# Where the second pass's features are transposed: score and value banks of PSUM in place of the products' ring, and a lead-in of six weave steps

## The chip, the core and the metric

The kernel runs on one core of one Trainium2 chip. The metric is the device time of one execution in microseconds; a measurement is the median of several executions. TensorE (PE in the profile) does the matrix products and the transposes, VectorE (DVE) and ScalarE (ACT) the elementwise work, GpSimd (POOL) a few subtractions, and the SP queue issues most of the transfers.

## What is computed

One layer of a hybrid step: attention and a matrix-memory scan side by side, one output projection, then a feed-forward network. There are 9 blocks of 128 tokens, one of context and eight latent ones, with a width of 1024. The parts that matter here are the last two of the layer:

```python
x = x + g1 * mix                          # mix: output projection of attention and scan
h2 = rmsnorm(x, norm2_w) * (1 + sc2) + sh2
x = x + g2 * swiglu(h2, w_gu, w_down)     # (silu(h2 @ w_g) * (h2 @ w_u)) @ w_down
```

## The kernel before

**Two passes of the feed-forward network.** The 9 blocks make 3 chunks of 3 blocks: `cur`, `nxt` and `far`. The feed-forward network of `cur` runs first, group by group of hidden columns: `gate_up` (24 products of 384 columns for each of two accumulators, lines 1473 to 1475 in `products`) and `down` (lines 1215 to 1217 in `three_blocks`). The chunks `nxt` and `far` follow together in a second pass, `pair6`, which forms a product of 2x2 blocks with seven block products in place of eight. It reads its right-hand operands, seven of them as pairs of fp16 parts, from the tile `Bt`.

**The features.** `Bt` is filled by `features6`, once for each of the six blocks of `nxt` and `far`. For each half of a block's 1024 columns it scales 512 columns on ACT into a buffer `t2` (line 1554), transposes them on PE in four pieces into a bank of PSUM (line 124, through the helper `transpose`), and copies the bank out with scale and shift into `F`: one quarter on ACT (line 1562), three on DVE (line 1564). Then ACT casts and DVE subtracts to make the two parts (lines 1569 and 145); a block of `far` also forms four sums T1 to T4 with its partner of `nxt` (lines 1578 to 1585).

**What runs beside it.** While groups of `cur` (from the fourth on) occupy PE, the generator `weave` takes side steps in proportion: first nothing for some steps, then the three blocks of `nxt`, then `attn_out` for `far` (its loads of spilled attention outputs into `t2` at line 1416, casts at 1418, products `out` at lines 1251 to 1255 and gated sums at 1204 and 1205, then row statistics at 1436 and the inverse root at 135 to 141), then the three blocks of `far`. The last heads of the attention for `far` (scores at line 1129, value products at 1153 and 1154) are still running as the first features come up. The program order made so is then moved by a scheduler, in which a `hot(n)` block goes ahead of other work by n.

**Banks.** PSUM has eight banks here: three for the attention's scores (`psum["S"]`, one tile of three banks), one for its value products (`psum["po"]`), and four that every other product takes in turn through `bank()`: gate-up, down, output projection, and the features' transposes.

**Buffers.** `t2` is a ring of three buffers of 2 KB a partition. The features' scaled halves, the gated sums, the loads at line 1416 and the scratch output of the weights' absolute sums (`jk`, line 178 in `load_piece`) share it. `F` and `T` lie in memory that the attention has used, so no `F` can be written before the attention's last output is through.

Of the kernel before, what the change touches and what calls it, by code (L numbers as in the profile page):

```python
# [8 lines left out]
F32 = mybir.dt.float32  # L9
# [10 lines left out]
P = 128  # L20
# [16 lines left out]
GROUPS = [(0, 4), (4, 4), (8, 4), (12, 5), (17, 5)]  # L37
# [5 lines left out]
NG = 3  # L43
# [6 lines left out]
def hybrid_step(ctx: ExitStack, tc: tile.TileContext, I: dict, O: dict):  # L50
# [8 lines left out]
    def hot(n):  # L59
        return tc.high_priority(n)  # L60

    def nm(s):
        uid[0] += 1
        return f"{s}_{uid[0]}"

    def weave(main, side, n_main, n_side):

        due = 0.0
        for units in main:
            due += n_side / n_main * (units or 1)  # L70
            while due >= 1.0:
                next(side, None)
                due -= 1.0

    def emit(gen):
        for _ in gen:
            pass

    def chain(*gens):
        for g in gens:  # L80
            for v in g:
                yield v
# [22 lines left out]
    psum = {"mm": es_b.enter_context(tc.tile_pool(name="pB", bufs=4, space=PSUM, reuse_waits="tile"))}  # L105
# [3 lines left out]
    def bank():  # L109
        turn_of[0] += 1  # L110
        at = psum["mm"] if "mm1" not in psum or turn_of[0] % 4 else psum["mm1"]
        return at.tile([P, 512], F32, name=nm("mm"), tag="mm")
# [10 lines left out]
    def transpose(out, in_, n=P):  # L123
        nc.tensor.transpose(out, in_, ident[:n, :n])
# [19 lines left out]
    def sub(out, full, hi, eng):  # L144
        (dve if eng == "dve" else pool).tensor_tensor(out=out, in0=full, in1=hi, op=ALU.subtract)  # L145
# [194 lines left out]
    ps = bank()  # L340
# [3 lines left out]
    ps = bank()  # L344
# [853 lines left out]
    def t2():  # L1198
        return ft.tile([P, 512], F32, name=nm("t2"), tag="t2", bufs=nt2[0])
# [206 lines left out]
    def attn_out(a, oT, row, home, spilled=None):  # L1406

        gs = row_pair(row)
        x1, parts = a["x1"], []
        for i in range(CB):  # L1410
            th, tl = home(i)
            parts.append((th, tl))
            o = oT[i]
            if spilled:
                o = t2().rearrange("p (k x) -> p k x", k=4)
                dma(o, spilled[i].rearrange("p (k x) -> p k x", k=4))
            with hot(500):
                nc.scalar.copy(th, o)
                sub(tl, o, th.bitcast(F32), "dve")
        for n in range(2):  # L1420
            with nullcontext() if spilled else tc.issue_after(loaded["turned"]):
                ws = out_pieces(0, n)
            for i, (th, tl) in enumerate(parts):
                ps = out_block([ws], 0, th, tl)
                with hot(200):
                    add_gated(x1[i], ps, gs[n], n)
                yield
        with hot(200):
            a["rs"] = stats(x1)
        yield  # L1430
# [46 lines left out]
    def gate_up(a, f0, nf):  # L1477
        th, tl = a["h2"]
        acts = a["act"] = []
        for f in range(f0, f0 + nf):  # L1480
            if True:
                pg, pu = bank(), bank()
                for off, ps in ((0, pg), (D_FF, pu)):
                    src = w_gu[f + (NF if off else 0)].rearrange("p (k n) -> p k n", k=KD)
                    wh, wl = load_piece([(full_view, src)], (KD, P), tally=2 * f + (off > 0))
                    products(ps[:, 0:CT], wh, wl, th, tl)
                    yield 6
                parts = [(slice(0, CT), pg[:, 0:CT], pu[:, 0:CT])]
            tn = fp.tile([P, CT], F32, name=nm("tn"), tag="tn", bufs=2)
            for cs, g, u in parts:  # L1490
                act(tn[:, cs], g, AF.Tanh, scale=0.5)
                dve.scalar_tensor_tensor(out=tn[:, cs], in0=tn[:, cs], scalar=1.0, in1=u, op0=ALU.add, op1=ALU.mult)  # L1492
                dve.tensor_tensor(out=tn[:, cs], in0=tn[:, cs], in1=g, op=ALU.mult)
            hl = hlp.tile([P, 2, CT], F32R, name=nm("hl"), tag="hl", bufs=5)
            ah, al = hl[:, 0], hl[:, 1]
            nc.scalar.copy(ah, tn)  # L1496
            sub(al, tn, ah.bitcast(F32), "pool")
            acts.append((ah, al))

    def down(c, a, f0, nf, n):  # L1500
        g = gate_bc(1, c, n)
        acts = a["act"]
        pieces = []
        for j in range(0, nf, 2):
            m = min(2, nf - j)
            rows = w_down[(f0 + j) * P : (f0 + j + m) * P, n * 512 : (n + 1) * 512].rearrange("(a p) n -> p a n", p=P)
            pieces.append(load_piece([(full_view, rows)], (m, 512)))
        yield from three_blocks(
            lambda k, i: (acts[k][0][:, i * P : (i + 1) * P], acts[k][1][:, i * P : (i + 1) * P]),
            pieces, nf, lambda i, ps: add_gated(a["x1"][i], ps, g(c * CB + i), n))  # L1510
# [35 lines left out]
    def features6(a, c, i, Bt, firsts):  # L1546

        x1, r = a["x1"][i], a["rs"][i]
        at = slice(i * P, (i + 1) * P)
        F = a4p.tile([P, KD, P], F32, name=nm("F"), tag="A4", bufs=7)  # L1550
        for half in range(2):
            with hot(600):
                y = t2()
                act(y, x1[:, half * 512 : (half + 1) * 512], AF.Copy, scale=r)
                ps = bank()
                for j in range(4):
                    transpose(ps[:, j * P : (j + 1) * P], y[:, j * P : (j + 1) * P])
                for j in range(4):
                    k = half * 4 + j
                    s, t = mods6[:, k, 0:1], mods6[:, k, 1:2]  # L1560
                    if j == 0:
                        act(F[:, k], ps[:, j * P : (j + 1) * P], AF.Identity, scale=s, bias=t)
                    else:
                        dve.tensor_scalar(out=F[:, k], in0=ps[:, j * P : (j + 1) * P], scalar1=s, scalar2=t, op0=ALU.mult, op1=ALU.add)
            yield
        for half, b in ((0, B11), (1, B21)) if c == 1 else ((1, B22),):
            v = F[:, half * 4 : half * 4 + 4]
            with hot(600):
                nc.scalar.copy(Bt[:, b, 0, :, at], v)
                sub(Bt[:, b, 1, :, at], v, Bt[:, b, 0, :, at], "dve")  # L1570
            yield
        if c == 1:
            firsts.append(F)
            return
        first = firsts.pop(0)
        T = sp.tile([P, 4, 4, P], F32, name=nm("T"), tag="S", bufs=1)
        with hot(600):
            dve.tensor_tensor(out=T[:, T1], in0=first[:, 0:4], in1=F[:, 0:4], op=ALU.subtract)
            dve.tensor_tensor(out=T[:, T2], in0=F[:, 4:8], in1=T[:, T1], op=ALU.add)
            dve.tensor_tensor(out=T[:, T3], in0=F[:, 0:4], in1=F[:, 4:8], op=ALU.subtract)  # L1580
            dve.tensor_tensor(out=T[:, T4], in0=first[:, 4:8], in1=T[:, T2], op=ALU.subtract)
        yield
        for j in (0, 2):
            with hot(600):
                nc.scalar.copy(Bt[:, j : j + 2, 0, :, at], T[:, j : j + 2])
                sub(Bt[:, j : j + 2, 1, :, at], T[:, j : j + 2], Bt[:, j : j + 2, 0, :, at], "dve")
            yield
# [162 lines left out]
    ps = bank()  # L1750
# [48 lines left out]
    def groups(c, a, lst):  # L1799
        for f0, nf in lst:  # L1800
            yield from gate_up(a, f0, nf)
            yield from down(c, a, f0, nf, 0)
            yield from down(c, a, f0, nf, 1)
# [3 lines left out]
    def mixing(tp, tag, bufs):  # L1807
        t = tp.tile([P, NQ, P], F32R, name=nm("mx"), tag=tag, bufs=bufs)
        return t[:, 0:4], t[:, 4:8]
# [7 lines left out]
    main = groups(0, cur, GROUPS[:NG])  # L1817
    with tc.issue_after(loaded["gate"]):
        for _ in range(4):
# [9 lines left out]
    Bt = btp.tile([P, 7, 2, 4, CT], F16, name="Bt")  # L1829
    firsts = []  # L1830
    feats = chain(*[features6(nxt, 1, i, Bt, firsts) for i in range(CB)],
                  attn_out(far, o2, g_d[0, 1], lambda i: mixing(a4p, "A4", 7), o_d[CB:]), *[features6(far, 2, i, Bt, firsts) for i in range(CB)])
    main = chain(groups(0, cur, GROUPS[NG:-1]), gate_up(cur, *GROUPS[-1]), down(0, cur, *GROUPS[-1], 0))
    weave(main, chain([None] * 10, feats), 18 * sum(nf for _, nf in GROUPS[NG:-1]) + 15 * GROUPS[-1][1], 54)
    emit(feats)
    main = down(0, cur, *GROUPS[-1], 1)
    next(main)
# [84 lines left out]
```

## Time and profile before

| | us |
|---|---|
| median of three runs | 1528.98 (1525.18 to 1530.79) |
| the profiled execution | 1527.74, of it the span 1526.0 |
| PE busy in the span | 1427.3 (94%) |
| DVE busy | 1129.1 (74%) |
| ACT busy | 813.6 (53%) |

The profiled execution is one execution with a hardware trace. Its page lists busy times, a timeline in 40 slices, the chain of work that ended last and the groups of instructions by line; the trace also answers who waited for whom, in which stretch, and what each engine did in order of time. Times within it count from the span's start. A group's idle time is what its engine stood still just before it. The granted clock is the share of TensorE's full clock that was allowed.

### The profile page before, as it was taken

Reading aid. Unit: us, or ns where it says so; the run is one execution under the profiler, and the core shown is the slowest. Engines: PE = TensorE matmul, PEld = TensorE weight load, DVE = VectorE, ACT = ScalarE, POOL = GpSimd, SP = SyncE. Lnnn points to the kernel's source line nnn. Section 1 sums busy time; section 2 is a strip of 40 time slices with the busy share of each in tenths; the row PEclk is TensorE's granted clock in tenths of the full one; section 3 lists DMA queues with packets and bytes.
Section 4 is the critical chain, followed back from the end, with each engine's and each line's share of the span. In section 5 each row is a group of like instructions: output and inputs, shape, how many; then the busy total and the mean of one; then the engine's idle time right before and its main releaser. Section 6 shows DMA issues by size and latency. Waiting matters only on the chain. (4 is left out here: it accounts for less than half of the span.)

```text
span 1526.0 us, 22787 instructions
## 1 busy us (share of the span) xinstructions
PE 1427.3 (94%) x8282; PEld 1064.8 (70%) x8282; DVE 1129.1 (74%) x2280; ACT 813.6 (53%) x1525; POOL 218.4 (14%) x310
## 2 busy tenths in 40 slices
PE   6889999998899889999999988989999999999994
PEld 3635667766677667978998977966766667676763
DVE  4978556775867878658678766969877696986857
ACT  5855467956767546555675944735233150523233
POOL 0122423232224335210100100100000000000000
PEclk9999999999999899999999999999999999999997
DMA  9575224553668764768687745334122130412112
GB/s 374 155 222 180 79 70 76 127 109 59 103 146 174 180 207 112 202 173 216 177 194 175 172 128 159 104 117 166 56 83 84 41 125 1 139 49 76 35 35 83
DMA packets 254182, 197.02 MB, mean 129 GB/s; under 512 B 166830, under 2 KB 208006, under 8 KB 254070
## 3 DMA queue, kind: packets, MB, share of 16 engines
q1 hardware_dynamic: 251070, 189.56, 45.8%
q10 hardware_dynamic: 2872, 5.62, 1.1%
q8 instruction: 65, 1.06, 0.3%
q14 instruction: 47, 0.39, 0.1%
q0 software_dynamic: 128, 0.39, 0.1%
HBM read 143.94 MB, written 13.26 MB: 103 GB/s over the span
## 5 line engine op out<-in xcount | busy, mean ns | idle before, releaser
L1621 PE MATMUL mm<-Bt,A 128*128 128x384 f16 x616 | 200.8, 326 | 0.0
L1620 PE MATMUL mm<-Bt,A 128*128 128x384 f16 x616 | 199.4, 326 | 0.5 <-DVE c L1641 0.5
L1622 PE MATMUL mm<-Bt,A 128*128 128x384 f16 x616 | 197.5, 326 | 0.0
L174 ACT CAST whi<-raw 128x1024 fp32r<-128x1024 f32 (+1 forms) x102 | 103.0, 1013 | 134.2 <-DMA raw<-in_w_down_dram 43.9
L145 DVE TENSOR_TENSOR wlo<-raw,whi 128x1024 fp32r<-128x1024 f32 (+1 forms) x102 | 121.3, 1190 | 52.9 <-ACT whi L174 50.5
L1136 DVE SCALAR_TENSOR_TENSOR pl<-pr,st,ph 128x1152 f16<-128x1152 f32 (+1 forms) x72 | 95.2, 1322 | 40.8 <-ACT ph L1135 40.8
L1473 PE MATMUL mm<-aTh,whi 128*128 128x384 f32 x352 | 121.3, 345 | 2.4 <-DVE tn L1492 1.2
L1474 PE MATMUL mm<-aTl,whi 128*128 128x384 f32 x352 | 120.2, 342 | 0.0
L1475 PE MATMUL mm<-aTh,wlo 128*128 128x384 f32 x352 | 120.0, 341 | 0.0
L1132 ACT ACTIVATE pr<-S,st 128x1152 f32<-128x1152 f32 (+1 forms) x72 | 81.5, 1132 | 51.8 <-DVE st L1131 50.5
L1131 DVE TENSOR_REDUCE st<-S 128x1 f32<-128x1152 f32 (+1 forms) x72 | 88.9, 1234 | 21.5 <-PE S L1129 21.4
L526 PE MATMUL wi<-headw,hT 128*128 128x384 f16 x288 | 93.9, 326 | 1.2 <-ACT th L816 1.2
L527 PE MATMUL wi<-headw,hT 128*128 128x384 f16 x288 | 93.9, 326 | 0.0
L528 PE MATMUL wi<-headw,hT 128*128 128x384 f16 x288 | 93.9, 326 | 0.0
L1135 ACT ACTIVATE ph<-pr,st 128x1152 f16<-128x1152 f32 (+1 forms) x72 | 83.7, 1163 | 17.1 <-DVE st L1134 8.5
L1129 PE MATMUL S<-kst,qT 128*128 128x384 f32 (+1 forms) x400 | 86.7, 350 | 3.6 <-ACT pr L1132 3.6
L1620 PEld LDWEIGHTS <-A 128*128 128x128 f16 x616 | 60.2, 98 | 42.5 <-issue 3.5
L1622 PEld LDWEIGHTS <-A 128*128 128x128 f16 x616 | 60.3, 98 | 39.8
L1621 PEld LDWEIGHTS <-A 128*128 128x128 f16 x616 | 60.3, 98 | 39.6 <-issue 0.6
L1606 ACT ACTIVATE A<-S,six 128x1024 f16<-128x1024 f32 x44 | 49.9, 1145 | 71.0 <-PE mm L1622 54.0
L1204 DVE TENSOR_TENSOR t<-mm,hmr 128x512 f32<-128x512 f32 x84 | 54.3, 683 | 41.0 <-PE mm L1690 33.3
L145 POOL TENSOR_TENSOR hl<-tn,hl 128x384 fp32r<-128x384 f32 x22 | 29.8, 1355 | 335.5 <-ACT hl L1496 307.9
(460 smaller groups left out, 3737.8 us busy)
## 6 DMA issues: line engine op xcount, KB each, us to landing
raw<-in_w_gu_dram SPq DMA_DIRECT2D x88, 512.0 KB, 3.4
raw<-in_w_down_dram SPq DMA_DIRECT2D x40, 512.0 KB, 3.8
a<-in_w_ada_dram SPq DMA_DIRECT2D x24, 512.0 KB, 5.6
iraw<-in_w_in_dram SPq DMA_DIRECT2D x32, 256.0 KB, 3.4
x<-in_x_sample_dram SPq DMA_DIRECT2D x11, 512.0 KB, 6.0
raw<-in_w_out_dram SPq DMA_DIRECT2D x10, 512.0 KB
aw<-in_w_ada_dram SPq DMA_DIRECT2D x8, 512.0 KB, 5.3
aw<-in_w_ada_dram SPq DMA_DIRECT2D x16, 256.0 KB, 7.8
```

Of the source, the lines that this page charges most:

```text
L145: (dve if eng == "dve" else pool).tensor_tensor(out=out, in0=full, in1=hi, op=ALU.subtract)
L174: nc.scalar.copy(hi[:, :n], raw[:, :n])
L526: mm(ps[:, :n], ah, wh[:, k % 2, c0 : c0 + n], start=(k == 0), stop=False)
L527: mm(ps[:, :n], ah, wl[:, k % 2, c0 : c0 + n], start=False, stop=False)
L528: mm(ps[:, :n], al, wh[:, k % 2, c0 : c0 + n], start=False, stop=(k == KD - 1))
L1136: dve.scalar_tensor_tensor(out=plv, in0=prv, scalar=st[:, 3:4], in1=phv, op0=ALU.mult, op1=ALU.subtract)
L1473: mm(ps, wh[:, k, :], th[:, k, :], start=(k == 0), stop=False)
L1474: mm(ps, wh[:, k, :], tl[:, k, :], start=False, stop=False)
L1475: mm(ps, wl[:, k, :], th[:, k, :], start=False, stop=(k == KD - 1))
L1620: mm(ps, wh[:, k], bt[:, 0, k], start=first and k == 0, stop=False, skip_group_check=True)
L1621: mm(ps, wh[:, k], bt[:, 1, k], start=False, stop=False, skip_group_check=True)
L1622: mm(ps, wl[:, k], bt[:, 0, k], start=False, stop=k == 3, skip_group_check=True)
```

## The change

Two edits. The features no longer take a bank from `bank()`. An even block (the first and third of a chunk) takes one tile `wide` of three banks from the score pool and uses one bank of it for each half; an odd block takes the value products' single bank for each half. And the side's lead-in is six empty steps instead of ten, with the weave's count of side steps lowered by the same to 48.

```diff
         F = a4p.tile([P, KD, P], F32, name=nm("F"), tag="A4", bufs=7)
+        wide = psum["S"].tile([P, 3, 512], F32, name=nm("S"), tag="S") if i % 2 == 0 else None
         for half in range(2):
             with hot(600):
                 y = t2()
                 act(y, x1[:, half * 512 : (half + 1) * 512], AF.Copy, scale=r)
-                ps = bank()
+                ps = wide[:, half] if i % 2 == 0 else psum["po"].tile([P, 512], F32, name=nm("po"), tag="po")
...
-    weave(main, chain([None] * 10, feats), 18 * sum(nf for _, nf in GROUPS[NG:-1]) + 15 * GROUPS[-1][1], 54)
+    weave(main, chain([None] * 6, feats), 18 * sum(nf for _, nf in GROUPS[NG:-1]) + 15 * GROUPS[-1][1], 48)
```

No instruction is added or taken away, but the scheduler writes another order. Lines after 1551 move down by one. In the rows below a name ends in the tile's number; `mm` is a bank of the ring, `S` the score tile, `po` the value bank, `t_2...` a scaled half in `t2`, `whi` and `wlo` the two parts of a weight piece.

PE before, at the end of the attention for `far`: the last group of value products (`po_9868`) has a feature's transposes on either side, and 24 gate-up products (`mm_10237`) behind.

```order
L1475 MATMUL mm_10236<-aTh_7241,wlo_10240 128x384
L124 MATMUL mm_10272<-ident,t_2038_10270 128x128 x4
...
L1153 MATMUL po_9868<-phT_9805,vs 128x256
...
L1154 MATMUL po_9868<-plT_9806,vs 128x256
L124 MATMUL mm_10220<-ident,t_2028_10218 128x128 x4
L1473 MATMUL mm_10237<-aTh_7241,whi_10284 128x384
```

PE at the same place in the changed program (`mm_10369` to `mm_10391` are down accumulators, `mm_10435` the first of the output projection for `far`):

```order
L1475 MATMUL mm_10249<-aTh_7241,wlo_10298 128x384
L1215 MATMUL mm_10369<-whi_10352,hl_9975 128x512
...
L1153 MATMUL po_9868<-phT_9805,vs 128x256
...
L1154 MATMUL po_9868<-plT_9806,vs 128x256
L1217 MATMUL mm_10369<-whi_10358,hl_10245 128x512
...
L124 MATMUL po_10187<-ident,t_2023_10185 128x128 x4
...
L124 MATMUL S_10086<-ident,t_2009_10097 128x128 x4
L124 MATMUL po_10198<-ident,t_2025_10196 128x128 x4
...
L124 MATMUL S_10285<-ident,t_2041_10286 128x128 x4
L124 MATMUL S_10285<-ident,t_2046_10328 128x128 x4
L1251 MATMUL mm_10435<-whi_10424,mx_10408 128x512 x2
```

All 48 gate-up products of this pair and 11 down products now stand ahead of the last value products. One group of transposes (the first half of `S_10086`) stands before them, 22 gate-up products ahead of the first down product; the other five groups stand behind, with 25, 3, 0, 6 and 0 down products before each, and the output projection follows the last group at once. Before, 33 down products stood between the last transposes and the output projection.

ACT before, from the last value products on: `F` is copied out of four banks that had been filled earlier.

```order
L1156 ACTIVATE ol_9887<-po_9868,vsc 64x256
L1562 ACTIVATE F_10117<-mm_10120,mods_6949 128x128
L1562 ACTIVATE F_10117<-mm_10172,mods_6949 128x128
L1562 ACTIVATE F_10217<-mm_10272,mods_6949 128x128
L1569 CAST Bt<-F_10117 128x4x128 x2
L1562 ACTIVATE F_10217<-mm_10220,mods_6949 128x128
...
L1418 CAST mx_10422<-t_2069_10423 128x512
```

ACT in the changed program, from the copy that follows the transposes into `po_10187`: the scaled halves `t_2041` and `t_2046` and three absolute sums `jk`, which had waited for buffers of `t2`, come in between, and the cast `mx_10408` that the output projection needs stands behind all of them.

```order
L1563 ACTIVATE F_10184<-po_10187,mods_6949 128x128
L178 ACTIVATE jk_10213,wsum<-whi_10208 128x1024
L1563 ACTIVATE F_10085<-S_10086,mods_6949 128x128
L178 ACTIVATE jk_10256,wsum<-whi_10251 128x1024
L1555 ACTIVATE t_2041_10286<-x_1388_6964,ry_8391 128x512
L1570 CAST Bt<-F_10184 128x4x128
L1563 ACTIVATE F_10184<-po_10198,mods_6949 128x128
L178 ACTIVATE jk_10302,wsum<-whi_10297 128x1024
L1555 ACTIVATE t_2046_10328<-x_1388_6964,ry_8391 128x512
...
L174 CAST whi_10430<-raw_10429 128x1024
...
L1418 CAST mx_10408<-t_2067_10409 128x512
```

On ACT's queue each of the two scaled halves shown now stands behind one or two sums, and 13 instructions stand between the first row and the cast for the output projection. On DVE a gated product of down (line 1204) and three copies to `F` from `po_10198` follow the subtraction for the first `Bt` row; from there to the read of `mm_10435` stand one gated add, four subtractions for `Bt`, three for `mx`, two times three copies, and four weight parts, one of them of half size.

PE before, at the first features of `far`, which need the statistics of the rows that the last output projection (`mm_10620`) completes:

```order
L1255 MATMUL mm_10620<-whi_10554,mx_10432 128x512 x2
L1473 MATMUL mm_10671<-aTh_7241,whi_10674 128x384
...
L1475 MATMUL mm_10671<-aTh_7241,wlo_10675 128x384
L124 MATMUL mm_10708<-ident,t_2132_10706 128x128 x4
L124 MATMUL mm_10719<-ident,t_2134_10717 128x128 x4
L1473 MATMUL mm_10672<-aTh_7241,whi_10729 128x384
```

PE at the same place in the changed program:

```order
L1255 MATMUL mm_10606<-whi_10543,mx_10418 128x512 x2
L1473 MATMUL mm_10681<-aTh_7241,whi_10684 128x384
...
L1475 MATMUL mm_10682<-aTh_7241,wlo_10727 128x384
L1473 MATMUL mm_10771<-aTh_7241,whi_10774 128x384
...
L1474 MATMUL mm_10771<-aTl_7242,whi_10774 128x384
L124 MATMUL S_10664<-ident,t_2123_10665 128x128 x4
L1475 MATMUL mm_10771<-aTh_7241,wlo_10775 128x384
```

There were 24 gate-up products between the end of the output projection and the first transposes of `far`; now there are 71. In the program as built, `mm_10671` lay in the bank of `mm_10620`, the accumulator just finished; `mm_10681` lies in a bank that was left long before, while `mm_10771` lies in the bank of `mm_10682`, which ends just before it. Likewise `mm_10479`, the third accumulator of the output projection, takes the bank of the first, `mm_10435`. The last transposes of `far` stood 72 gate-up products ahead of the last down products; now 6 stand there.

## The prediction

> **What bounds the kernel now.** PE is busy for 1427.3 of 1526.0 us, so I looked for the stretch where it is not, around the change: which waits of PE end there, by what, and how long. First the list of PE's waits from 840 to 1023 us, where the features are made (in us: total, times, longest):
>
> ```profile
> PE mm L124 <- ACT t L1554: 5.1, 1, 5.1
> PE mm L204 <- DVE pv L193: 2.7, 1, 2.7
> PE mm L124 <- DVE F L1564: 2.5, 1, 2.5
> PE po L1153 <- DMA phT<-ph: 1.5, 1, 1.5
> PE mm L1215 <- DVE tn L1492: 1.3, 1, 1.3
> PE mm L1473 <- DVE tn L1492: 1.2, 2, 0.9
> PE po L1154 <- DMA plT<-pl: 1.0, 1, 1.0
> PE mm L1473 <- DVE t L1204: 0.9, 1, 0.9
> PE mm L1215 <- DVE t L1204: 0.9, 1, 0.9
> PE mm L1473 <- DVE F L1564: 0.3, 1, 0.3
> ```
>
> They sum to 17.4 us. Next the busy times of the stretches (columns: stretch, length, busy time and count of PE, PEld, DVE, ACT, POOL, then granted clock, DMA share, GB/s):
>
> ```profile
> 840.00:1023.00 183.00, 165.50 (x866) 147.99 (x865) 131.27 (x215) 107.01 (x165) 14.96 (x10) 0.96 0.46 130
> 894.80:898.40 3.60, 3.54 (x11) 3.57 (x12) 3.60 (x9) 2.49 (x5) 0.00 (x0) 0.53 0.00 0
> 950.00:970.00 20.00, 20.00 (x114) 19.94 (x113) 17.22 (x30) 19.73 (x35) 1.53 (x1) 0.93 0.33 106
> 1015.00:1023.00 8.00, 8.00 (x26) 5.96 (x27) 4.23 (x8) 6.02 (x8) 0.00 (x0) 0.61 0.19 54
> 911.80:939.00 27.20, 27.20 (x119) 21.68 (x117) 18.53 (x26) 8.48 (x12) 0.00 (x0) 1.00 0.45 142
> ```
>
> PE stands still for 17.5 us of these 183, and after a cluster of waits it also runs slower: at a clock of 0.53 for 3.6 us, which costs 0.47 x 3.6 = 1.7 us, and at 0.93 over 20 us, 1.4 us. From 911.8 to 939 it does 119 products of 512 columns without a gap, 0.23 us each. ACT is full (19.73 of 20) from 950 to 970.
>
> Last the two worst places in order of time. The end of the attention (start, length, engine, line, and in brackets the idle time before it):
>
> ```profile
> 891.97 1.16 ACT L1562 ACTIVATE F<-mm,mods 128x128 f32<-128x128 f32 x3
> 892.71 2.96 DVE L1564 TENSOR_SCALAR F<-mm,mods 128x128 f32<-128x128 f32 x9
> 893.90 0.63 PE L124 MATMUL mm<-ident,t 128*128 128x128 f32 x4 [2.47 <-DVE F L1564]
> 899.80 0.34 PE L1474 MATMUL mm<-aTl,whi 128*128 128x384 f32 x1
> 899.97 0.33 PE L1475 MATMUL mm<-aTh,wlo 128*128 128x384 f32 x1
> ```
>
> Copies to `F` start at 891.97 on ACT and at 892.71 on DVE, when the last value output is out and its memory may be written; the three halves that these copies read have kept their banks until then. The fourth group waits 2.47 us for a bank, with 24 gate-up products behind it. (Two of those start 0.17 us apart.) And the first features of `far`:
>
> ```profile
> 939.90 0.41 PE L1473 MATMUL mm<-aTh,whi 128*128 128x384 f32 x1 [0.88 <-DVE t L1204]
> 947.23 0.16 DVE L141 SCALAR_TENSOR_TENSOR ry<-rt,ry 128x3 f32<-128x3 f32 x1
> 947.71 1.04 ACT L174 CAST whi<-raw 128x1024 fp32r<-128x1024 f32 x1 [2.83 <-DMA raw<-in_w_gu_dram]
> 948.66 1.33 ACT L1554 ACTIVATE t<-x,ry 128x512 f32<-128x512 f32 x2
> 949.43 0.81 PE L124 MATMUL mm<-ident,t 128*128 128x128 f32 x3 [5.14 <-ACT t L1554]
> ```
>
> After 24 products PE meets transposes whose statistics are not done, and on ACT a weight cast that waits for its transfer stands ahead of the scaled half.
>
> **What goes.** (1) Features hold none of the ring's four banks, so gate-up products no longer wait for them: 1.2 us (line 1473 for line 1492) goes. (2) The value products now stand behind 24 more gate-up products (24 x 0.17 = 4.1 us) and 11 down products (2.5 us). Their transposing transfers, 1.5 and 1.0 us late today, are covered; without that cover they cost 2.5 us. (3) No gate-up product stands behind a transpose that waits for `F`: 2.5 + 0.3 = 2.8 us, and with (1) and (2) the slow clock behind that cluster, 1.7 us. (4) `mm_10681` takes a bank long free: 0.9 us at 939.90. (5) 71 instead of 24 products cover the statistics of `far`: 47 x 0.17 = 8.0 us more, against 5.1 us of wait and 1.4 us of clock, 6.5 us. In the new order DVE's line 1492 (on `mm_10682`) stands ahead of the last step of the root, so the scaled half comes about as late as now; the cover holds with some 3 us over. (6) The last gate-up accumulators end in time for down: 1.3 us.
>
> Sum: 1.2 + 2.5 + 2.8 + 1.7 + 0.9 + 6.5 + 1.3 = 16.9 us. Two waits stay as they are: 0.9 us for line 1204 and 2.7 us for line 193, since the rows around them keep their order. The 48 transposes and their copies cost what they cost; the SP queue only issues a few weight transfers in another order, POOL has none of the moved work.
>
> **What comes instead.** The new waits are not in the trace, so I follow the new order by start distances of rows like them. ACT:
>
> ```profile
> 950.94 1.03 ACT L174 CAST whi<-raw 128x1024 fp32r<-128x1024 f32 x1
> 951.87 0.45 ACT L1562 ACTIVATE F<-mm,mods 128x128 f32<-128x128 f32 x1
> 952.23 1.05 ACT L178 ACTIVATE jk<-whi 128x1024 bf16<-128x1024 f32 x1
> ...
> 953.27 1.04 ACT L178 ACTIVATE jk<-whi 128x1024 bf16<-128x1024 f32 x1
> ...
> 954.65 1.33 ACT L1554 ACTIVATE t<-x,ry 128x512 f32<-128x512 f32 x2
> 955.88 1.05 ACT L178 ACTIVATE jk<-whi 128x1024 bf16<-128x1024 f32 x1
> ...
> 957.86 0.63 ACT L1569 CAST Bt<-F 128x512 f16<-128x512 f32 x1
> 958.38 0.46 ACT L1562 ACTIVATE F<-mm,mods 128x128 f32<-128x128 f32 x1
> ```
>
> A weight cast takes 0.93, a copy to `F` 0.36, a sum 1.04, a scaled half 0.62 (1.23 for two), a cast to `Bt` (and to `mx`, of the same size) 0.52. DVE:
>
> ```profile
> 959.14 1.22 DVE L145 TENSOR_TENSOR wlo<-raw,whi 128x1024 fp32r<-128x1024 f32 x1
> 960.28 0.69 DVE L145 TENSOR_TENSOR Bt<-F,Bt 128x512 f16<-128x512 f32 x1
> 960.88 1.05 DVE L1564 TENSOR_SCALAR F<-mm,mods 128x128 f32<-128x128 f32 x3
> 961.84 1.22 DVE L145 TENSOR_TENSOR Bt<-T,Bt 128x1024 f16<-128x1024 f32 x1
> ```
>
> A weight's second part takes 1.14, three copies to `F` 0.96, a subtraction of 512 columns 0.60. The other instructions of 512 columns on DVE I take at 0.60 too.
>
> Let 0 be the end of the last value product. PE does 25 down products (5.8 us) and one group of transposes (0.4, an estimate from the 0.63 at 893.90 less its overlap), until 6.2. ACT from there: copy, sum, copy, sum, half: `t_2041` is out at 6.2 + 0.36 + 1.04 + 0.36 + 1.04 + 0.62 = 9.6. PE, with 9 down products and two groups, is there at 9.1 and waits **0.5**. ACT goes on with cast, copy, sum, half: `t_2046` at 9.6 + 0.52 + 0.36 + 1.04 + 0.62 = 12.1; PE is ready at 10.0 and waits **2.1**. Then cast, copy, weight cast, cast, weight cast, `mx` cast: 12.1 + 0.52 + 0.36 + 0.93 + 0.52 + 0.93 + 0.52 = 15.9; PE ends its transposes at 12.5 and waits **3.4** for the output projection's operand. Its first 24 products run until 21.4. The next accumulator lies in the bank of the first, which DVE reads only after its backlog. From the `Bt` cast at 10.1 DVE does a subtraction, a gated product and three copies: 10.1 + 0.60 + 0.60 + 0.96 = 12.3. Then nine operations of 0.60, two times three copies and three weight parts, and the read itself: 12.3 + 5.4 + 1.9 + 3.4 + 0.6 = 23.6, and PE waits **2.2**. Farther on, `mm_10771` waits for the bank of `mm_10682` as line 1473 did for line 1492 today: **0.9**.
>
> That gives back 0.5 + 2.1 + 3.4 + 2.2 + 0.9 = 9.1 us. Each of these could be nothing, if ACT gets to its queue earlier than I place it, and each could be up to twice that, if the transfers behind the weight casts are late as the 2.83 us at 947.71; so 0 to 18 us, and I take the 9.1 since it rests on the steps of the same instructions. A slow clock after the 3.4 us wait would lengthen the 24 products by the 1.7 us of the cluster above, but PE waits 2.2 us for DVE right behind them, so that hides it.
>
> The trace halved the clock for 3.6 us after waits none of which is over 2.5 us. [...]
>
> Net: 16.9 - 9.1 = 7.8 us off the profiled execution's 1527.74, 1519.9. It lies 1.24 us below the median of the runs, so in terms of the median 1528.98 - 7.8 = **1521.2 us**. What is won before the second pass reaches the end, since PE has next to no gap in it, though DVE is nearly full:
>
> ```profile
> 1023.00:1100.00 77.00, 76.48 (x429) 50.54 (x428) 69.91 (x112) 33.31 (x42) 0.00 (x0) 1.00 0.39 135
> ```
>
>
> **Rivals.** A measurement of this kernel can tell about 0.5% from no change, 7.6 us.
>
> *The waits come back smaller.* If ACT and DVE reach their queues early and nothing is given back, the gain is all 16.9: 1512.1. For it: ACT has 76 us free of the 183. Against: the sums `jk` cannot move ahead of the transposes that free their buffers.
>
> *Nothing to measure.* The output projection begins no sooner than now, since its operand hangs on the chain from the attention's last head through ACT, not on PE, and the clock falls in the middle as it does at 1015 (0.61 over 8 us, 3.1 us). Then 7.8 - 3.1 - 1.7 = 3.0 us remain: 1526.0. For it: in my steps ACT's chain ahead of the projection has no gap left. [...]
>
> *Slower.* Each half's transposes need the value or score bank emptied and a scaled half that stands behind sums on ACT. If all six halves of `nxt` were paid one by one, each would cost copy, sum, copy, sum, half, cast: 0.36 + 1.04 + 0.36 + 1.04 + 0.62 + 0.52 = 3.9 us, 23.6 in all, less the 34 down products between (7.8): 15.8 in place of the 2.6 that I count before the projection, 13.2 more; with the 3.1 us of slow clock that such waits bring, 16.3 more, against a gain of 7.8: 8.5 us longer, 1537.5. It decides from the point at which the first four halves wait too. Against it: the order sets one group far ahead and 25 down products before the next. A tail does not get there alone: the last features and the last gated sums of down stand so today:
>
> ```profile
> 988.70 1.21 DVE L145 TENSOR_TENSOR Bt<-T,Bt 128x1024 f16<-128x1024 f32 x1
> 1005.82 0.69 DVE L1204 TENSOR_TENSOR t<-mm,gx 128x512 f32<-128x512 f32 x1 [1.40 <-PE mm L1217]
> ```
>
> That is 15.9 us of room, of which 66 gate-up products (11.2 us) go; 4.7 us are left before features hold up the weights' scale.
>
> **How the numbers follow.** The forecast has 0.46; its own range is 1517 to 1525.5, about half on either side of the 7.6 us, so 0.25 faster and 0.21 the same. All waits gone: 0.18, faster. Nothing to measure: 0.24, same. Slower: 0.12. That makes faster 0.43, same 0.45, slower 0.12. The range of 8 in 10 reaches from 1514, which leaves out the lower half of the first rival, to 1530.5, which leaves out the slower one.
>
> **What would show it.** Right: no wait of PE for phT, plT or `F` at the end of the attention; behind it PE's waits for ACT t of about 0.5 and 2 us, one of some 3 us for mx, one of 2 us for line 1204, and none at the first transposes of `far`; the gated sum that starts at 1005.82 starts near 998. Wrong: a wait for t at `far`'s transposes still over 2 us, or more than 12 us of waits between the last value products and the end of the output projection, or new waits behind 960 us, where ACT was full.

## The result and the profile after

| | before | changed |
|---|---|---|
| median | 1528.98 us (1525.18 to 1530.79) | 1519.19 us (1516.65 to 1522.59) |
| ratio to before, 95% interval | | 0.994 (0.9918 to 0.9962) |
| the profiled execution | 1527.74 us, span 1526.0 | 1519.19 us, span 1517.4 |

Both medians are of five executions. The changed kernel takes 0.4 to 0.8% less time. The forecast was 1521.2 us. PE's waits from 840 to 1023 us in the changed kernel, in the columns of the first list of the prediction:

```profile
PE S L124 <- DVE F L1565: 4.4, 1, 4.4
PE mm L204 <- DVE pv L193: 3.3, 1, 3.3
PE mm L1251 <- ACT mx L1418: 1.0, 1, 1.0
PE mm L1473 <- DVE tn L1492: 0.7, 1, 0.7
PE po L124 <- DVE F L1565: 0.6, 1, 0.6
PE mm L1251 <- ACT whi L174: 0.6, 1, 0.6
PE mm L1215 <- DVE t L1204: 0.5, 1, 0.5
```

They sum to 11.1 us against 17.4. (Lines behind 1551 are one higher than before.) The waits for phT, plT and `t` are gone; the longest one now is that of a feature's transposes in the score tile for copies to `F`. The stretch of that wait and the three behind it, with the granted clock third from the end, show what it brings:

```profile
903.10:907.45 4.35, 0.00 (x0) 0.01 (x1) 4.35 (x11) 3.93 (x7) 0.00 (x0) 1.00 0.71 244
907.45:909.40 1.95, 0.99 (x4) 0.61 (x4) 1.95 (x3) 1.59 (x3) 0.00 (x0) 0.54 0.77 288
909.40:912.90 3.50, 3.48 (x8) 2.80 (x9) 3.50 (x8) 2.03 (x5) 0.00 (x0) 0.50 0.87 293
912.90:916.40 3.50, 3.50 (x13) 2.75 (x13) 3.08 (x5) 2.05 (x3) 0.00 (x0) 0.78 0.06 10
```

The transposes behind the wait run at 0.54, the projection's first products at half clock for 3.5 us and at 0.78 for as long again: 0.50 x 3.5 + 0.22 x 3.5 = 2.5 us. In order of time, the end of the last value product and what PE waits for until the projection:

```profile
892.21 0.27 PE L1154 MATMUL po<-plT,vs 128*128 128x256 f16 x1
900.38 0.63 PE L124 MATMUL po<-ident,t 128*128 128x128 f32 x4 [0.60 <-DVE F L1565]
907.47 0.99 PE L124 MATMUL S<-ident,t 128*128 128x128 f32 x4 [4.39 <-DVE F L1565]
909.42 2.07 PE L1251 MATMUL mm<-whi,mx 128*128 128x512 f32 x4 [0.96 <-ACT mx L1418]
921.52 0.74 PE L1251 MATMUL mm<-whi,mx 128*128 128x512 f32 x2 [0.55 <-ACT whi L174]
```

Far's first features, a row of ACT and a row of PE, and a gated sum of down:

```profile
949.13 0.73 ACT L1555 ACTIVATE t<-x,ry 128x512 f32<-128x512 f32 x1 [1.27 <-DVE ry L141]
953.18 0.60 PE L124 MATMUL S<-ident,t 128*128 128x128 f32 x4
997.86 0.69 DVE L1204 TENSOR_TENSOR t<-mm,gx 128x512 f32<-128x512 f32 x1 [1.23 <-PE mm L1217]
```

The scaled half is out at 949.9 and its transposes come up at 953.2, so the cover holds with 3.3 us over.

### The profile page after: what moved, and what is told of

Its sections match the earlier page's. It is cut to its first block, busy times and chain, and to the rows that moved or that the text cites. A ratio compares the mean times of both kernels' runs of the same rounds, so it can differ in the third digit from the quotient of the medians.

```text
span 1517.4 us, 22777 instructions
## 1 busy us (share of the span) xinstructions
PE 1424.7 (94%) x8282; PEld 1062.5 (70%) x8282; DVE 1130.1 (74%) x2280; ACT 812.2 (54%) x1525; POOL 216.2 (14%) x310
## 4 chain that ended last, share of the span: by engine, by line
PE 57%; DVE 5%; ACT 3%; DMA 2%; issue 1%; POOL 0%; SPq 0%; ACTq 0%; DVEq 0%; POOLq 0%
PE mm L1621 7%; PE mm L1623 7%; PE mm L1622 7%; PE mm L1689 4%; PE mm L1690 4%; PE mm L1691 4%; PE mm L1473 3%; PE mm L1475 3%; PE mm L1474 3%; PE mm L1215 2%; PE mm L1216 2%; PE mm L1217 2%; PE S L1129 2%; PE mm L1251 1%; PE mm L1253 1%
## 5 line engine op out<-in xcount | busy, mean ns | idle before, releaser
L1689 PE MATMUL mm<-whi,hl 128*128 128x512 f32 x192 | 76.8, 400 | 0.0
```

The lines of the kernel that those rows point to most:

```text
L1689: mm(ps, hl[:, 0, sl], wh[:, k % 2, :], start=(k == 0), stop=False)
```

## The experiments

The theory that I set down ahead of these runs, "banks": the features no longer hold the ring's banks, so products can stand where waits were. Its rivals: the earlier weave does it ("delay"), only the products ahead of far's first transposes do it ("cover"), or the end of the attention does it. Times are medians; the ratio is to the kernel before, timed beside it on the same chip, with a 95% interval.

### Banks and delay apart

The changed kernel with the old weave:

```diff
-    weave(main, chain([None] * 6, feats), ..., 48)
+    weave(main, chain([None] * 10, feats), ..., 54)
```

Expected: 

> The new banks with the old delay of ten steps and 54 side steps. Theory 'banks' (what pays is that no feature holds one of the ring's four banks, and that gate-up and down products can therefore be put where waits were): most of the gain is kept, 1518 to 1523 us. Theory 'delay' (the earlier weave is what moves the output projection and the far features ahead, the banks are beside the point): the gain is gone, 1526 to 1531 us. In its order the first transposes of far stand behind 79 gate-up products, so by 'banks' PE waits there for no scaled half.

Measured 1517.51 us, ratio 0.9944 (0.9926 to 0.9963). That is 0.5 us below the range of "banks": the whole gain is there without the shorter delay, and at far's first transposes PE waits for nothing.

The kernel before with the new weave (the same two numbers the other way round):

Expected: 

> The old ring of banks with the new delay of six steps and 48 side steps. Theory 'banks': no gain, 1525 to 1532 us, since the halves still hold the ring's banks, and the first transposes of far stand right behind the last down group with no gate-up product ahead of them, so PE waits there about 6 us for the scaled half (5.1 us with 24 gate-up products of 4.2 us as cover before; now 15 down products of 3.5 us). Theory 'delay': 1517 to 1522 us.

Measured 1527.83 us, ratio 1.0 (0.9989 to 1.0011). The wait at far's first transposes is 5.3 us, where I had said about 6:

```profile
PE mm L124 <- ACT t L1554: 5.3, 1, 5.3
```

So the delay brings nothing, with the ring or without it. "Delay" falls.

### The two places apart

Score and value banks for `nxt` alone, the ring for `far`; and the other way round:

```diff
-        wide = psum["S"].tile(...) if i % 2 == 0 else None
+        wide = psum["S"].tile(...) if (c == 1) and i % 2 == 0 else None
...
-                ps = wide[:, half] if i % 2 == 0 else psum["po"].tile(...)
+                ps = bank() if not (c == 1) else wide[:, half] if i % 2 == 0 else psum["po"].tile(...)
```

(`c` is 1 for `nxt` and 2 for `far`; `tile(...)` is shortened here.) Expected of `nxt` alone: 

> New delay; the score and value banks only for the three blocks of nxt, the ring for the three of far. The order up to the end of the output projection is that of the changed kernel, then 24 gate-up products stand ahead of far's first transposes. By my steps the 5.1 us wait and the 1.4 us of slow clock there come back, 6.5 us: 1525 to 1527 us. By the rival 'the gain is made at the end of the attention, far's cover is beside the point': 1518 to 1521 us.

Measured 1527.67 us, ratio 1.0004 (0.9993 to 1.0014), 0.7 us above my range. At far's first transposes PE waits for the half, and the gate-up products behind them then wait for the copies that free a bank of the ring; the clock is halved behind that:

```profile
PE mm L124 <- ACT t L1555: 3.4, 1, 3.4
PE mm L1473 <- DVE F L1565: 2.4, 1, 2.4
```

```profile
953.50:957.10 3.60, 3.49 (x12) 3.43 (x13) 2.30 (x3) 3.60 (x8) 0.00 (x0) 0.50 0.45 134
957.10:960.70 3.60, 3.60 (x17) 3.60 (x17) 2.53 (x6) 3.60 (x8) 0.00 (x0) 0.72 0.20 82
```

Expected of `far` alone (`c == 2` in the diff): 

> New delay; the ring for the three blocks of nxt, the score and value banks for the three of far. 47 gate-up products (8.0 us) stand ahead of far's first transposes, against 24 (4.1 us) before, so of the 5.1 us wait 1.2 is left, and the slow clock behind it goes: by my steps 5 us less than the kernel that differs from it only in far's banks (old ring, new delay) or more, and with the attention's end as before 1521 to 1526 us. By the rival 'the gain is made at the end of the attention': as slow as before, 1526 to 1531 us.

Measured 1519.98 us, ratio 0.9953 (0.9938 to 0.9968): the gain of the full change as nearly as this can be told. All of it is made at far's transposes; the new banks at the attention's end gain nothing by themselves.

### Cover without banks

The kernel before, with two empty steps ahead of far's features:

```diff
-                  attn_out(far, ...), *[features6(far, 2, i, Bt, firsts) for i in range(CB)])
+                  attn_out(far, ...), [None] * 2, *[features6(far, 2, i, Bt, firsts) for i in range(CB)])
-    weave(main, chain([None] * 10, feats), ..., 54)
+    weave(main, chain([None] * 10, feats), ..., 56)
```

Expected: 

> The kernel before (ring, delay of ten) with two empty weave steps ahead of far's features and two more side steps, so that 48 instead of 24 gate-up products (8.2 instead of 4.2 us) stand ahead of far's first transposes, with the ring's banks kept. Theory 'cover' (only the products ahead of far's first transposes count, in whatever bank): of the 5.1 us wait about 1 us is left, 1521 to 1525 us. Theory 'banks' (with the ring, gate-up products behind the transposes wait for the copies to F that hold the banks, so the cover cannot be had that way): 1526 to 1530 us.

Measured 1521.28 us, ratio 0.995 (0.9935 to 0.9965). The wait for `t` is 0.2 us, while the longest wait at the attention's end is as before:

```profile
PE mm L124 <- DVE F L1564: 2.5, 1, 2.5
PE mm L124 <- ACT t L1554: 0.2, 1, 0.2
```

My theory "banks" falls for this place: 48 products ahead of the transposes do what the change does, with the ring kept. Item (5) of the prediction had put the gain there down to those products too. The banks were the means by which the order came to have 71 there.

### What holds the output projection

The changed kernel, each block's halves in two different tiles:

```diff
-        wide = psum["S"].tile(...) if i % 2 == 0 else None
...
-                ps = wide[:, half] if i % 2 == 0 else psum["po"].tile(...)
+                ps = psum["S"].tile([P, 3, 512], ...)[:, 0] if half == 0 else psum["po"].tile(...)
```

Expected: 

> The changed kernel, but each block's first half goes into a score tile of its own and its second half into the value bank, so that no two halves of one block share a tile. In the changed kernel the sixth half of nxt waits 4.4 us for the copies of the fifth, which lie in the same score tile. Theory 'that wait is covered' (the output projection's operand, which ACT casts at the same time, ends no sooner): as the changed kernel, 1517 to 1521 us, with a longer wait for mx in place of the shorter one for F. Theory 'that wait is paid': 2 to 4 us less, 1514 to 1517 us.

Measured 1519.79 us, ratio 0.9945 (0.9928 to 0.9962), no different from the changed kernel. The wait of the sixth half is 2.2 us in place of 4.4, and what it loses the wait for mx gains:

```profile
PE mm L1251 <- ACT mx L1418: 3.9, 1, 3.9
PE po L124 <- ACT Bt L1569: 2.2, 1, 2.2
```

So the 4.4 us wait, the longest in the list, is covered: the projection's operand is what ends last. In the changed kernel that operand's path reads so (queue SP, then ACT):

```profile
904.12 0.34 SPq L1416 DMA_DIRECT2D t<-o_d  x1
```

```profile
907.81 1.05 ACT L174 CAST whi<-raw 128x1024 fp32r<-128x1024 f32 x1 [0.78 <-DMA raw<-in_w_down_dram]
908.76 0.61 ACT L1418 CAST mx<-t 128x512 fp32r<-128x512 f32 x1
```

Its load goes out at 904.12, as a sum on ACT ends (904.10) and a buffer of the `t2` ring comes free, and the cast stands behind a weight cast. Next, the load goes straight into the operand, without a `t2` buffer:

```diff
-                o = t2().rearrange("p (k x) -> p k x", k=4)
+                o = tl.bitcast(F32)
                 dma(o, spilled[i].rearrange("p (k x) -> p k x", k=4))
```

Expected: 

> The changed kernel, but the attention's output for the second projection is loaded straight into the low part of its operand mx and split there, not into the three buffers that it shares with the scaled halves and the weights' sums. Theory 'chain' (the projection starts late because these loads wait for the halves' buffers): the projection starts 3 to 5 us sooner after the last value product than the changed kernel's 16.9 us, the slow clock behind it goes, 1512 to 1516 us. Theory 'ACT is full there anyway': 1518 to 1521 us.

Measured 1516.85 us, ratio 0.9917 (0.9899 to 0.9936), by its interval not yet apart from the changed kernel's. The three loads now go out from 896.31, 8.9 us after the last value product (which ends at 887.38), where the first went out 11.6 us after it, and the projection starts 14.6 us after it, against 16.9:

```profile
896.31 1.37 SPq L1416 DMA_DIRECT2D mx<-o_d  x3
```

```profile
900.38 1.04 ACT L174 CAST whi<-raw 128x1024 fp32r<-128x1024 f32 x1
901.31 0.63 ACT L1418 CAST mx<-mx 128x512 fp32r<-128x512 f32 x1
```

```profile
901.99 1.71 PE L1251 MATMUL mm<-whi,mx 128*128 128x512 f32 x4 [4.02 <-ACT mx L1418]
```

I had expected 3 to 5 us sooner and no slow clock; it was 2.3 us, PE still waits 4.0, and the clock is 0.56 for the 3.5 us behind it. ACT works from 895 to 902 without a gap, and the cast stands at the end of its queue. So the buffers were a part of it, and the queue is the rest.

The same loads with the ring for `nxt`, where 45 down products stand ahead of the projection:

Expected: 

> Score and value banks for far only, ring for nxt, and the direct loads. With the ring PE has 45 down products ahead of the projection and waits nowhere for mx, so by theory 'chain' the direct loads change nothing: 1518 to 1522 us, as without them. Theory 'loads on the queue delay weights': 1515 to 1518 us.

Measured 1522.02 us, ratio 0.9956 (0.9941 to 0.9972): no gain, since nothing waits for mx there.

### A version that beats both

Direct loads, and the operand of far's first two blocks (load, cast, subtraction) written ahead of the features of `nxt` in the program; the third block's after them:

```diff
-    feats = chain(*[features6(nxt, 1, i, Bt, firsts) for i in range(CB)], attn_out(far, ...), ...)
+    feats = chain(heads(), *[features6(nxt, 1, i, Bt, firsts) for i in range(CB)], rest(), ...)
```

(Not shown: `heads()` writes load, cast and subtraction of two blocks, `rest()` is `attn_out` for `far` with the third.)

Expected: 

> The kernel with direct loads, and the loads and casts of the second projection's operand for its first two blocks stand ahead of the features of nxt in the program (the third block's after them, as before). On ACT two of the mx casts now stand right behind the first copy to F, ahead of the sums and the scaled halves. Theory 'ACT's queue' (the projection starts late because mx is cast behind copies, sums, halves and weight casts): it starts about 8 us after the last value product instead of 14.6, no slow clock behind it, 4 to 6 us less than with the direct loads alone, 1510 to 1514 us. Theory 'another wait takes its place' (weights of the projection, or its accumulators read late by DVE): 1515 to 1519 us.

Measured 1510.95 us, ratio 0.9885 (0.9863 to 0.9907). On ACT the casts of mx (line 1411 here) now stand ahead of the sums (line 178) and halves, and the projection starts 8.4 us after the last value product (889.65), without a wait:

```profile
894.12 0.62 ACT L1411 CAST mx<-mx 128x512 fp32r<-128x512 f32 x1 [3.48 <-DMA mx<-o_d]
895.17 0.62 ACT L1411 CAST mx<-mx 128x512 fp32r<-128x512 f32 x1
895.87 0.46 ACT L1564 ACTIVATE F<-po,mods 128x128 f32<-128x128 f32 x1
896.23 1.05 ACT L178 ACTIVATE jk<-whi 128x1024 bf16<-128x1024 f32 x1
```

```profile
898.08 1.18 PE L1251 MATMUL mm<-whi,mx 128*128 128x512 f32 x4
```

All of PE's waits from 840 to 1022 us:

```profile
PE mm L204 <- DVE pv L193: 3.3, 1, 3.3
PE mm L1215 <- DVE t L1204: 0.9, 2, 0.7
PE mm L1251 <- DVE t L1204: 0.8, 1, 0.8
PE mm L1216 <- DVE wlo L145: 0.6, 1, 0.6
PE mm L1251 <- ACT whi L174: 0.2, 1, 0.2
```

5.8 us in place of the changed kernel's 11.1. All three blocks early:

Expected: 

> The same with all three blocks' operands ahead of the features. The third block's attention output is written only after the last value product, so its cast may hold ACT's queue until the transfer there and back has landed. Theory 'ACT's queue': 1510 to 1514 us, as with two, or 1 to 3 us more where that transfer holds it. Theory 'another wait takes its place': 1515 to 1519 us.

Measured 1511.25 us, ratio 0.9891 (0.9874 to 0.9908), the same as with two.

Last, whether the banks are needed for this: the kernel before with its ring and delay, 48 products ahead of far's transposes, and the two operands early.

Expected: 

> The kernel before with its ring and its delay of ten, plus what helped elsewhere: 48 gate-up products ahead of far's first transposes, direct loads, and two blocks' operands early. Theory 'the banks still pay' (with the ring the waits at the attention's end stay, about 8 us with their slow clock, and PE has 42 down products ahead of the projection anyway): no faster than with the ring and the cover alone, 1519 to 1523 us, against 1511 with banks and early operands. Theory 'the banks are beside the point': 1510 to 1515 us.

Measured 1520.02 us, ratio 0.9943 (0.9924 to 0.9962). The ring's waits at the attention's end are all there:

```profile
PE mm L124 <- DVE F L1565: 2.5, 1, 2.5
PE po L1153 <- DMA phT<-ph: 1.3, 1, 1.3
PE po L1154 <- DMA plT<-pl: 1.2, 1, 1.2
PE mm L1474 <- DVE tn L1493: 0.9, 1, 0.9
```

The four rows and 0.3 us more lie at the attention's end, 6.2 us, and the clock behind them is at 0.57 for 3.6 us, another 0.43 x 3.6 = 1.5 us:

```profile
895.80:899.40 3.60, 3.26 (x12) 3.05 (x13) 2.74 (x8) 1.58 (x4) 0.00 (x0) 0.57 0.53 186
```

Of what else differs, 0.7 us is a wait at far's transposes and 1.3 us one of down for gate-up's accumulators. So of the 9 us between this kernel and the one with the two operands early, most is at the attention's end: the new banks (here with the delay of six) do pay there, once the projection's operand no longer ends last. In the changed kernel that gain is there and is given back.

## Why the prediction was right

**What goes, 16.9 us: every wait named is gone.** None of the six items is left in the list of waits after: no wait for phT, plT or `t`, the first gate-up product after the projection follows it at once, and down waits for no gate-up accumulator. The 71 products cover far's half with 3.3 us over, where I had said some 3.

**What stays, 3.6 us:** 0.5 for line 1204 and 3.3 for line 193, 3.8 together.

**What comes, 9.1 us: the size near, the cause right for two of the five waits.** Ahead of the projection I had 0.5 + 2.1 + 3.4 = 6.0; it was 0.60 + 4.39 + 0.96 = 5.95. What I had right is that ACT's chain sets the end: the copy that it begins with starts 6.2 after the last value product, as placed, and the operand is out at 16.9 where I had 15.9, of which 0.78 is a weight's transfer. That the waits agree to 0.05 us is luck: the operand came 1.0 us later, and PE's own work ahead of it took 16.9 - 5.95 = 11.0 us in place of 15.9 - 6.0 = 9.9, since four of its five groups of transposes took 0.6 us or more, the last 0.99 at the slow clock, where I had estimated 0.4. How PE's idle time divides along that chain I had wrong. The step that failed was to let each half wait for its scaled input on ACT only. PE waited for neither half; the waits of 0.60 and 4.39 us were both for copies to `F`. The two halves of a `wide` tile lie in different banks, but the second half's transposes still waited for the copies of the first; the row of DVE that ended the 4.39 us wait is

```profile
906.28 1.04 DVE L1565 TENSOR_SCALAR F<-S,mods 128x128 f32<-128x128 f32 x3
```

which ends at 907.32, 0.15 us before the transposes start; with the halves in different tiles this wait ended sooner and the time stayed. Two other terms traded places, which is luck too. The 2.2 us for the read of the first accumulator did not come: the third accumulator waited for nothing. I had let that wait hide the slow clock; without it, the 2.5 us of slow clock are paid in full, with a wait of 0.55 for a weight cast. `mm_10771` waited 0.7, where I had 0.9. Altogether 5.95 + 0.55 + 2.5 + 0.7 = 9.7 came back.

**The sum.** 16.9 - 9.7 - 0.2 = 7.0 us by the list. From the first product of the second pass to the span's end both kernels take the same within 0.7 us, and that product starts at

```profile
1013.70 0.34 PE L1621 MATMUL mm<-Bt,A 128*128 128x384 f16 x1
```

against 1021.60 before, 7.9 us earlier. All of it lies in the stretch that I added up: the scores that start at 852.9 start within 0.02 us of each other, and from there to that product PE takes 160.8 us in place of 168.7 and is idle for 11.0 in place of 17.5. (The attention's last scores end 1.2 us earlier, at 877.4 against 878.6. That is moved work: two groups of transposes, at 862.80 and 871.64, stand ahead of them in the kernel before and behind them in the changed one.) So the stretch gives 7.9 us where the forecast was 7.8, while the list with its measured terms gives 7.0; the 0.9 us between them is not placed, and that much of the agreement is luck. The difference of the medians, 9.8 us, has the spread of the runs in it besides.

**The places.** By my own terms the attention's end gives (1) to (3), 8.2 us, and gets back 0.5 + 2.1 + 3.4 + 2.2 = 8.2: nothing; the gain is (4) to (6) less 0.9. I did not say so, but the experiments do: `nxt` alone 1.0004, `far` alone 0.9953. With `nxt` alone, that is with `far` put back into the ring, the way from those scores (854.42 there) to the second pass takes 167.8 us. That is 0.9 less than before, and 7.0 more than with the change, where (4) and (5) less the 0.9 say 6.5. The wait for the half is shorter there than before, 3.4 us in place of 5.1, but with the ring the products behind the transposes waited 2.4 us for the copies too. (The medians differ by 8.5 us and the spans by as much; in the profiled executions 1.55 us of that is there at the scores already, ahead of the features.)

**The rivals.** "The waits come back smaller" did not happen in the changed kernel; the last kernels show what it would take, the operand early on ACT, and 1511 us is near the 1512.1 that I had worked out for it. "Nothing to measure" was wrong on the whole but right on its mechanism: the projection hangs on ACT's chain, which from its first copy at 898.69 had no gap but the 0.78 us, and the clock did fall there, at a cost of 2.5 us where it had 3.1. The 1.7 us that its sum takes off besides, the slow clock of before, the run does not show: up to the wait of 4.39 us the clock is 1.00. In "Slower", the waits paid one by one did not come, since only the sixth half waited long.

**The signs.** Of those that I had named, these came: no wait for phT or plT, none at the first transposes of `far`, and the gated sum at 997.86. Missed were no wait for `F` (it is the longest), two waits for ACT t (none came), some 3 us for mx (0.96) and 2 us for line 1204 (none in the projection). None of the signs of being wrong came: the waits from the last value product to the projection's end are 6.5 us, against my bound of 12.

**The clock.** I took the halved clock of before as the work of several short waits, with 1.7 us of the gain hanging on it; the 1.7 us did go, with the waits: the granted clock of the changed kernel is 1.00 from the end of the last value product, at 892.48, to 903.10. Then it fell behind one wait of 4.39 us, to 0.54 and then 0.50; in the first of the two runs below it fell to 0.54 behind waits of 2.52 us and less.

## What to carry to other kernels

Ask for each wait of the busiest engine whether what it leads to would have come any sooner without it: the longest wait in the changed kernel was free to remove, and worth nothing (4.39 us cut to 2.2, and 1519.79 us against 1519.19), because the next operand was on another engine's queue. When a change frees a resource and the time hardly moves, look for the chain that now ends last, shorten that, and try the change again: here the banks gained nothing at the attention's end until the operand's loads left the shared buffers and two casts were moved ahead in ACT's queue, and then most of 9 us. And where work must wait for a chain of statistics, first try to put more products ahead of it: two empty steps in the weave bought what the bank change did (ratio 0.995 against 0.994).

## What the runs showed of the hardware that was not expected

The length of the longest wait did not by itself decide whether the clock fell. Two kernels with the same last and longest wait of 2.52 us at the attention's end differ in the two waits before it, 1.44 and 0.91 us in the one, 0.84 and 0.92 in the other. The stretch with the waits and the one behind, ring with the new delay first, far alone second:

```profile
875.80:885.50 9.70, 4.88 (x40) 3.77 (x37) 5.17 (x10) 5.57 (x11) 0.00 (x0) 1.00 0.73 168
885.50:889.10 3.60, 3.45 (x12) 3.11 (x13) 3.60 (x11) 2.15 (x5) 0.00 (x0) 0.54 0.11 40
```

```profile
875.90:885.20 9.30, 5.02 (x42) 3.92 (x40) 4.67 (x10) 5.50 (x10) 0.00 (x0) 1.00 0.69 163
885.20:888.40 3.20, 2.87 (x17) 2.66 (x18) 3.20 (x10) 2.01 (x4) 0.00 (x0) 1.00 0.10 36
```

With 4.82 us of the 9.70 idle the clock was 0.54 afterwards; with 4.28 of 9.30 it stayed at 1.00. Whether the sum of the idle time decides these runs do not tell.
